# A hybrid decoder layer: the first tile of tokens gathers its own rows of U before it meets V densely

## The chip, the cores and the metric

The kernel runs on one NeuronCore of a Trainium2 chip. The metric is device microseconds from the first to the last instruction of one execution, as the median of timed runs. The engines are TensorE (PE in the profile, its weight loads PEld), VectorE (DVE), ScalarE (ACT), GpSimd (POOL) and SyncE (SP, which issues most DMAs).

## The reference, cut to what matters

The layer has two sub-layers over 512 tokens of width 1024. The first is token mixing by two groups of attention heads; the change doesn't touch it. The second is a retrieval over 128 x 128 = 16384 single-neuron experts:

```python
q = (hc @ w_q).reshape(-1, PEER_HEADS, PEER_KEY_DIM)     # 8 heads, 128 wide
s1 = einsum('chd,nd->chn', q[..., :half], k1)             # 128 keys on each side
s2 = einsum('chd,nd->chn', q[..., half:], k2)
v1, i1 = top_k(s1, 16); v2, i2 = top_k(s2, 16)
cand_s = v1[..., :, None] + v2[..., None, :]
best_s, best_pos = top_k(cand_s, 16)                      # 16 experts per head, 128 per token
expert = i1 * 128 + i2 at best_pos
g = softmax(best_s)
act = gelu(einsum('cd,chkd->chk', hc, u[expert]))         # rows of U
out = einsum('chk,chkd->cd', g * act, v[expert])          # rows of V
```

So each token uses 128 rows of U (16384 x 1024, f32) and the same 128 rows of V. The result, times a gate, is added to the residual and normalised.

## The kernel before, in words

The 512 tokens are four tiles of 128. Tiles 0, 1 and 2 are dense (`ND` = 3, `DT` = 384 tokens): for them every expert is computed and weighed by a gate matrix G that is zero where a token did not choose an expert. Tile 3 is sparse: for each of its 128 (head, choice) pairs an indirect DMA issued on GpSimd fetches one row of U per token, VectorE forms the dot product with the token's `h2n` row, and later a row of V is fetched and added into `acc0` on VectorE.

Every product in high precision is split into a high and a low float32r part (`hi` on ScalarE, `lo = raw - hi` on VectorE or GpSimd), and `mm3` (lines 147 to 150) issues three matmuls for each pair of operands.

The second sub-layer runs in this order:

1. Queries (`p_q`) of all tiles, and `route` (both sides' top 16 and the top 16 of their sums, on VectorE).
2. `choose` turns the lists into key numbers and gates (`sel3`). `spread` and `hot` (lines 781 to 816) build one-hot factors on VectorE, `gates` (line 820) multiplies them on TensorE into G and stores it to DRAM (`g_d`), 8 groups of 16 tokens for each of three dense tiles. Among these lie blocks of U: `u_block` (line 863) loads 128 experts' rows of U, splits them (`uhi`, `ulo`; `UPOOL` names the 14 blocks split on GpSimd), multiplies them with 384 tokens (24 matmuls of 128 x 384) and applies gelu. 56 blocks (`NAHEAD`) are done here; the first 16 (`NSPILL`) are written to DRAM, 40 stay in SBUF.
3. V, block by block (`v_load`, `v_mm`, lines 965 to 1004): 128 rows of V are split (`vhi`, `vlo`), the block's activations are weighed (`w = a * G`), split (`wh`, `wl`) and multiplied: 18 matmuls of 128 x 512 into six accumulators. From V block 16 on, one of the 72 remaining blocks of U goes with each block of V. The gathers of tile 3 are spread over the V blocks by the rates `RATE`: `due` counts up, and each whole number emits one gather with its VectorE operation.

The tile framework orders each engine's instructions once, when the program is built; `issue_after` keeps a gather's VectorE operation behind the last `wl`, and `high_priority` lets the load and the split of a block of U run ahead.

Of the kernel before, what the change touches and what calls it, by code (L numbers as in the profile page):

```python
# [9 lines left out]
F32 = mybir.dt.float32  # L10
# [47 lines left out]
UPOOL = tuple(range(0, 56, 4))  # L58
# [12 lines left out]
# columns of the small projection group  # L71
# [4 lines left out]
def hybrid_layer(ctx: ExitStack, tc, x, pos, wada, wada_n, cols, w_small, w_in_a, w_in_b, wuk, wuv,  # L76
# [19 lines left out]
    a_d = [dram.tile([P, DT], F32, name=f"a_d{b}") for b in range(NSPILL)]  # L96
# [70 lines left out]
    def row_out(s, pl, tag, bufs=1):  # L167
        """Section s of the modulation as one row in DRAM."""
# [22 lines left out]
    # ------------------------------------------------------------------ adaLN: mod = silu(c) @ w_ada + b_ada  # L191
# [17 lines left out]
    def mod_section(s, tiles, k0=0):  # L209
        """One section of the modulation; tiles holds [rows of w_ada's transpose, one column block each], loaded already or to load."""  # L210
# [10 lines left out]
    def mod_tiles(s, pl, tags, n, bufs=1):  # L221
        """The rows of a section, n blocks to a tile, with the tags in turn."""
# [7 lines left out]
    # the first two sections wait for their products where later tiles will lie; TensorE takes half of the first  # L230
# [12 lines left out]
    # x, normalised and transposed, before the modulation is known  # L243
# [44 lines left out]
    # ------------------------------------------------------------------ rotary tables  # L288
# [22 lines left out]
    def rope(v, nh, half, cs, sn, name):  # L311
        """v [P, NT, nh, >= 2*half], in place."""
# [12 lines left out]
    # ------------------------------------------------------------------ combined projection  # L325
# [69 lines left out]
    # queries, keys and values of group A; keys and values from the latent  # L395
# [26 lines left out]
    def forget():  # L422
        """Running sum of log sigmoid, as extra rows of keys and queries."""
# [30 lines left out]
    # queries, keys and values of group B  # L454
# [19 lines left out]
    # ------------------------------------------------------------------ attention  # L474
# [128 lines left out]
    # ------------------------------------------------------------------ group B, output projection, residual and PEER norm, tile by tile  # L603
# [19 lines left out]
    def peer_norm(j, x1):  # L623
        """h2 of tile j, transposed and split."""
# [19 lines left out]
    def h2_of(i, j):  # L644
        return h2l[0][:, i] if j == NT - 1 else h2[i][:, :, j * P:(j + 1) * P]
# [13 lines left out]
    for qt in range(NT):  # L659
# [4 lines left out]
        if qt == 1:  # L664
            h2 += [h2p.tile([P, KC, DT], F32R, tag=f"h2_{i}", name=f"h2_{i}") for i in range(2)]
# [8 lines left out]
    # ------------------------------------------------------------------ PEER: queries  # L674
    hp_ = opened(ctx, "hp")
    h2n = hp_.tile([P, D], F32, name="h2n")
    acc0 = hp_.tile([P, D], F32, name="acc0")
    g0 = hp_.tile([P, P], F32, name="g0")
    e0 = hp_.tile([P, P], U32, name="e0")
    w0 = hp_.tile([P, P], F32, name="w0")  # L680
    dot0 = hp_.tile([P, P], F32, name="dot0")
    if MB:
        row_out(5, hp_, "g4", 4)
    qT = [hp_.tile([P, PH, P], F32, tag="g4", name=f"qT{j}", bufs=4) for j in range(NT)]
    h2l.append(wo.tile([P, 2, KC, P], F32R, tag="mt", name="h2l", bufs=2))
    hf = peer_norm(NT - 1, x1s[NT - 1])
    for k4 in range(2):
        tp = one(f"tp_h2n{k4}")
        for k in range(4):
            nc.tensor.transpose(tp[:, k * P:(k + 1) * P], hf[:, k4 * 4 + k, :], ident)  # L690
        nc.scalar.activation(h2n[:, k4 * 512:(k4 + 1) * 512], tp, AF.Copy)
# [3 lines left out]
    # ------------------------------------------------------------------ PEER: product keys  # L695
# [6 lines left out]
    def route(n, j, idx, bval, bpos):  # L702
        """Product keys of heads 4n..4n+3 for the tokens of tile j."""
# [34 lines left out]
    def choose(j, idx, bval, bpos):  # L738
        """The two key numbers and the gate of each of the 128 (head, choice) pairs."""
# [41 lines left out]
    def spread(j, sel3):  # L781
        """One-hot factors: second key numbers as columns; first ones as 8 x 16, the gate in two parts on the 8."""
        i1 = rp.tile([P, 3, P], I32, tag="i1", name=f"i1_{j}")
        nc.vector.tensor_copy(i1[:, 0], sel3[:, 0])
# [5 lines left out]
        for i, src in enumerate((f1[:, 0], f1[:, 1], sel3[:, 1], sel3[:, 2])):  # L790
            nc.tensor.transpose(tp[:, i * P:(i + 1) * P], src, ident)
        tt = rp.tile([P, 5, P], F16, tag="tt", name=f"tt{j}")
        nc.scalar.activation(tt[:, 0:3], tp[:, 0:3 * P].rearrange("p (i t) -> p i t", t=P), AF.Copy)
        nc.scalar.activation(tt[:, 3], tp[:, 3 * P:4 * P], AF.Copy, scale=GSCALE)
        nc.vector.scalar_tensor_tensor(tt[:, 4], tp[:, 3 * P:4 * P], GSCALE, tt[:, 3], op0=ALU.mult, op1=ALU.subtract)
# [24 lines left out]
    def gates(j, tg, half, oh):  # L820
        """G[i2, i1, t] of these tokens; to DRAM 16 tokens at a time."""
# [3 lines left out]
        for t4 in range(2):  # L825
            o = one(f"p_g{j}_{tg}_{half}_{t4}", "pl")
            for t in range(4):
                q, e = divmod(t4 * 4 + t, 2)
                for i in (1, 0):
                    nc.tensor.matmul(o[:, t * P:(t + 1) * P], oh[2][:, q, :, e], oh[i][:, q, :, e],  # L830
                                     start=(t == 0 and i == 1), stop=i == 0, skip_group_check=True)
            ts_ = slice(half * 8 + t4 * 4, half * 8 + t4 * 4 + 4)
            nc.scalar.activation(st[:, :, ts_].rearrange("p i t -> p t i"), o.rearrange("p (t i) -> p t i", i=NK),  # L833
                                 AF.Copy, scale=1.0 / GSCALE)
# [5 lines left out]
    for n in range(2):  # L840
        his, los = wchunks(wo, [w_pq[n]], 512, f"pq{n}", 16, 2)
        for j in range(NT):
            o = one(f"p_q{n}_{j}", "pl")
            for k in range(KC):
                mm3(o, h2_of(0, j)[:, k], h2_of(1, j)[:, k], his[k], los[k], k == 0, k == KC - 1)
            qn = wo.tile([P, 512], F32, tag="x1", name=f"qn{n}_{j}", bufs=2)
            nc.scalar.activation(qn, o, AF.Copy)
            tp = one(f"tp_q{n}_{j}", "pj")
            for h in range(4):
                nc.tensor.transpose(tp[:, h * P:(h + 1) * P], qn[:, h * P:(h + 1) * P], ident)  # L850
# [268 lines left out]
```

## Time and profile before

| quantity | value |
|---|---|
| timed runs | 1632.31, 1643.91, 1644.44 us; median 1643.91 |
| span of the profiled execution | 1631.3 us (the profile gives no own time apart from the span; the lowest timed run is 1.0 us above it) |
| TensorE busy | 1549.9 us, 95% of the span |
| VectorE busy | 1273.8 us, 78% |
| ScalarE busy | 694.4 us, 43% |
| GpSimd busy | 538.3 us, 33% |
| moved by DMA | 383.39 MB, 235 GB/s over the span |
| mean granted TensorE clock | 0.967 of full speed |

Busy times of one engine can't be added to those of another, since the engines run side by side. Matmul records overlap each other, so the pace of TensorE is read from the distance between two starts, not from the length of a record; the same holds for VectorE, whose records overlap by some 0.08 us.

### The profile page before, as it was taken

To read this page: it belongs to the slowest core of one execution; us is meant where nothing else is said; L and a number is where in the kernel's file an instruction comes from. 1 tells how busy PE (TensorE), PEld (TensorE's weight loads), DVE (VectorE), ACT (ScalarE), POOL (GpSimd) and SP (SyncE) were. 2 spreads that over 40 slices of the span, in tenths; PEclk is the share of its full clock that TensorE was granted. 3 is DMA by queue.
4 is the path that set the end of the run, shared out by engine and by line. 5 is a ranking of instruction groups with operands and counts; after the bars stand their busy time and mean duration, and the time that the engine had idled before them with its cause. 6 is when DMAs were issued, how large, how long until landed. Compare 5 with 4: busy or idle time off the path is not lost.

```text
span 1631.3 us, 23016 instructions
## 1 busy us (share of the span) xinstructions
PE 1549.9 (95%) x8200; PEld 1348.3 (83%) x8202; DVE 1273.8 (78%) x2639; ACT 694.4 (43%) x1110; POOL 538.3 (33%) x406
## 2 busy tenths in 40 slices
PE   6889999998988998999999999999999999999997
PEld 5756777776788888888888999999999999988885
DVE  7898753655999999994468888878878888868886
ACT  4553434444334774865433333333333333333333
POOL 2344202213011202041005554555455445534420
PEclk7999898799999999999999999999999999999999
DMA  8643002413034655575889999989989899879974
GB/s 336 209 153 121 23 27 66 154 65 119 27 106 150 209 196 168 209 266 213 291 270 324 363 337 335 359 308 352 326 331 354 311 348 337 313 279 320 315 257 155
DMA packets 152899, 383.39 MB, mean 235 GB/s; under 512 B 11712, under 2 KB 66384, under 8 KB 149456
## 3 DMA queue, kind: packets, MB, share of 16 engines
q1 hardware_dynamic: 114912, 246.45, 44.3%
q0 software_dynamic: 36864, 134.23, 21.9%
q8 instruction: 64, 1.05, 0.3%
q10 hardware_dynamic: 1008, 1.24, 0.2%
q14 instruction: 51, 0.42, 0.1%
HBM read 349.36 MB, written 32.51 MB: 234 GB/s over the span
## 4 chain that ended last, share of the span: by engine, by line
PE 51%; DVE 3%; DMA 2%; issue 1%; ACT 1%; SPq 0%; POOL 0%; DVEq 0%; POOLq 0%; ACTq 0%
PE acc L1003 30%; PE p_u L150 7%; PE p_u L149 7%; PE p_u L148 7%; DMA ar<-a_d 1%; DVE gu L910 1%; DMA u<-in_ut_dram 1%; PE p_g L830 0%; DVE oh L814 0%; ACT st L833 0%; DMA v<-in_pv_dram 0%; DVE vlo L982 0%; DVE ulo L870 0%; DVE o L1024 0%; DVE x1b L1016 0%
## 5 line engine op out<-in xcount | busy, mean ns | idle before, releaser
L148 PE MATMUL p_u<-h,uhi 128*128 128x384 f32 x1024 | 349.1, 341 | 1.3 <-ACT a L876 1.3
L150 PE MATMUL p_u<-h,ulo 128*128 128x384 f32 x1024 | 348.6, 340 | 0.7 <-DVE ulo L870 0.6
L149 PE MATMUL p_u<-h,uhi 128*128 128x384 f32 x1024 | 348.1, 340 | 0.0
L902 POOL DMA_INDIRECT gu<-in_un_dram,e x128 | 192.0, 1500 | 297.3 <-DVE gu L910 203.5
L869 ACT ACTIVATE uhi<-u 128x1024 fp32r<-128x1024 f32 x128 | 135.8, 1061 | 292.3 <-PE p_u L149 247.6
L902 POOL DMA_INDIRECT gv<-in_pv_dram,e x128 | 191.7, 1498 | 205.2 <-DVE acc L921 155.2
L1003 PE MATMUL acc<-vhi,wh 128*128 128x512 f32 x768 | 237.3, 389 | 1.7 <-ACT wh L995 1.1
L1003 PE MATMUL acc<-vlo,wh 128*128 128x512 f32 x768 | 237.5, 389 | 0.8 <-DVE vlo L982 0.8
L1003 PE MATMUL acc<-vhi,wl 128*128 128x512 f32 x768 | 237.0, 389 | 0.0
L148 PEld LDWEIGHTS p_u<-h,uhi 128*128 128x128 f32 x1024 | 194.6, 190 | 4.7 <-ACT a L876 1.7
L149 PEld LDWEIGHTS p_u<-h,uhi 128*128 128x128 f32 x1024 | 195.0, 190 | 2.9
L150 PEld LDWEIGHTS p_u<-h,ulo 128*128 128x128 f32 x1024 | 194.7, 190 | 1.7 <-DVE ulo L870 1.0
L995 ACT ACTIVATE wh<-w 128x384 fp32r<-128x384 f32 x128 | 67.3, 526 | 299.9 <-issue 181.2
L996 DVE TENSOR_TENSOR wl<-w,wh 128x384 fp32r<-128x384 f32 x128 | 71.4, 558 | 136.7 <-ACT wh L995 136.6
L870 DVE TENSOR_TENSOR ulo<-u,uhi 128x1024 fp32r<-128x1024 f32 x114 | 139.0, 1219 | 48.9 <-ACT uhi L869 32.2
L1003 PEld LDWEIGHTS acc<-vlo,wh 128*128 128x128 f32 x768 | 144.0, 188 | 31.6 <-DVE vlo L982 1.7
L1003 PEld LDWEIGHTS acc<-vhi,wl 128*128 128x128 f32 x768 | 144.2, 188 | 29.9
L921 DVE SCALAR_TENSOR_TENSOR acc<-gv,w,acc 128x1024 f32<-128x1024 f32 x127 | 162.4, 1279 | 5.8 <-DMA gv<-in_pv_dram,e 5.5
L910 DVE SCALAR_TENSOR_TENSOR gu<-gu,h2n 128x1024 f32<-128x1024 f32 x128 | 158.6, 1255 | 9.7 <-DMA gu<-in_un_dram,e 9.7
L1003 PEld LDWEIGHTS acc<-vhi,wh 128*128 128x128 f32 x768 | 143.2, 188 | 26.7 <-ACT wh L995 1.4
L982 DVE TENSOR_TENSOR vlo<-v,vhi 128x1024 fp32r<-128x1024 f32 x128 | 156.1, 1220 | 5.0 <-ACT vhi L981 5.0
L981 ACT ACTIVATE vhi<-v 128x1024 fp32r<-128x1024 f32 x128 | 135.5, 1058 | 12.3 <-DMA v<-in_pv_dram 5.0
(356 smaller groups left out, 2396.3 us busy)
## 6 DMA issues: line engine op xcount, KB each, us to landing
u<-in_ut_dram SPq DMA_DIRECT2D x128, 512.0 KB, 5.3
v<-in_pv_dram SPq DMA_DIRECT2D x128, 512.0 KB, 5.9
g_d<-st SPq DMA_DIRECT2D x24, 1024.0 KB, 4.7
gt<-g_d SPq DMA_DIRECT2D x48, 512.0 KB, 8.8
wada<-in_wada_dram SPq DMA_DIRECT2D x12, 1024.0 KB, 4.9
raw_b<-in_w_in_b_dram SPq DMA_DIRECT2D x12, 512.0 KB, 3.6
x<-in_x_dram SPq DMA_DIRECT2D x8, 512.0 KB, 4.4
raw_o<-in_w_out_dram SPq DMA_DIRECT2D x8, 512.0 KB, 3.5
```

Of the source, the lines that this page charges most:

```text
L148: nc.tensor.matmul(o, ahi, bhi, start=start, stop=False, **kw)
L149: nc.tensor.matmul(o, ahi, blo, start=False, stop=False, **kw)
L150: nc.tensor.matmul(o, alo, bhi, start=False, stop=stop, **kw)
L869: nc.scalar.activation(hi, raw, AF.Copy)
L870: (nc.gpsimd if b in UPOOL else nc.vector).tensor_tensor(lo, raw, hi.bitcast(F32), op=ALU.subtract)
L902: nc.gpsimd.indirect_dma_start(out=t, out_offset=None, in_=src, in_offset=bass.IndirectOffsetOnAxis(ap=e0[:, s:s + 1], axis=0))
L910: nc.vector.scalar_tensor_tensor(t, t, 1.0, h2n, op0=ALU.mult, op1=ALU.mult, accum_out=dot0[:, s:s + 1])
L921: nc.vector.scalar_tensor_tensor(acc0, t, w0[:, s:s + 1], acc0, op0=ALU.mult, op1=ALU.add)
L981: nc.scalar.activation(hi, raw, AF.Copy)
L982: nc.vector.tensor_tensor(lo, raw, hi.bitcast(F32), op=ALU.subtract)
L996: last[0] = nc.vector.tensor_tensor(wl, w, wh.bitcast(F32), op=ALU.subtract).ins
L1003: nc.tensor.matmul(accs[2 * j + n], l[:, js], r[:, n * 512:(n + 1) * 512], start=b == 0 and i == 0, stop=b == NK - 1 and i == 2)
```

## The change

Tile 0 becomes half sparse. As soon as its experts are chosen, 128 indirect DMAs fetch its rows of U, VectorE forms the dots, and gelu and gate make `w0[0]`. Its matrix G then holds the finished weights, gate times activation, not the gates. So the dense products with U take tiles 1 and 2 alone (`UT` = 256 tokens), while V still meets tiles 0, 1 and 2. G of tile 0 is built last, from three bf16 parts in place of two f16 parts of the value. The queries are all computed before the blocks of U, tile 0 is routed first, and one more tile is routed among the blocks of U. 72 blocks of U are done ahead of V (`NSPILL` is 32). Half of the U splits (`UPOOL`, 64 of 128) and 30 of the V splits (`VPOOL`) go to GpSimd. In the V stage the weighing is done in place in the tile of G, and only for 256 tokens.

```diff
 ND = NT - 1
 DT = ND * P
+UT = DT - P
 NACT = 40
-NSPILL = 16
+NSPILL = 32
 NAHEAD = NACT + NSPILL
-WHEN = ((0, 2), (3, 5))
+WHEN = (1, 4)
-NGP = (0, 0, 0, 0, 1, 2, 3, 3)
+NGP = (1, 1, 2, 2, 2, 2, 2, 2)
-GPAT = (2, 2, 2, 2, 2, 2, 2, 2)
+GPAT = (3, 3, 3, 3, 3, 3, 3, 3)
+EARLY = (16, 6, 8)
-UPOOL = tuple(range(0, 56, 4))
+UPOOL = tuple(range(0, 128, 2))
+VPOOL = tuple(range(2, 120, 4))
...
+    query(0, 0)
+    route(0, 0, *lists[0])
+    query(1, 0)
+    route(1, 0, *lists[0])
+    query(0, 1)
+    query(1, 1)
+    sel3 = choose(0, *lists[0])
+    experts(0, sel3)
...
-        o = psum(f"p_u{b}")[:, :DT]
+        o = psum(f"p_u{b}")[:, :UT]
...
-        t = hp_.tile([P, D], F32, tag="g4", name=f"{name}{s}", bufs=4)
+        t = hp_.tile([P, D], F32, tag="g4", name=f"{name}{s}", bufs=6)
...
+    def dot(i, s, name):
+        t = gathered(un, i, s, name)
+        with tc.issue_after(last[0]) if last[0] is not None else nullcontext():
+            nc.vector.scalar_tensor_tensor(t, t, 1.0, h2n[i], op0=ALU.mult, op1=ALU.mult, accum_out=dot0[i][:, s:s + 1])
...
     u_ahead(U0[0])
+    dots(EARLY[0] // 2)
+    route(0, 1, *lists[1])
+    route(1, 1, *lists[1])
     u_ahead(U0[1])
+    dots(EARLY[0] // 2)
+    sel3 = choose(1, *lists[1])
...
+    for i, (j, coming) in enumerate(((1, 2), (2, 3), (0, None))):
+        if j == 0:
+            dots(TOPK)
+            weighed(0, slice(0, P))
+            tt = spread(0, sel0[:, 0], sel0[:, 1], w0[0])
+        else:
+            tt = spread(j, sel3[:, 0], sel3[:, 1], sel3[:, 2])
...
+                if tg == WHEN[0]:
+                    route(0, coming, *lists[coming])
+                    route(1, coming, *lists[coming])
...
+                dots(EARLY[1 + i])
             u_ahead(GPAT[tg])
...
-        nc.vector.tensor_tensor(lo, raw, hi.bitcast(F32), op=ALU.subtract)
-        w = vp.tile([P, DT], F32, tag="w", name=f"w{b}", bufs=2)
+        (nc.gpsimd if b in VPOOL else nc.vector).tensor_tensor(lo, raw, hi.bitcast(F32), op=ALU.subtract)
...
+        gw = gts[0][:, :, :, b % 8, :].rearrange("p j g t -> p (j g) t")
+        nc.vector.tensor_tensor(gw[:, P // 16:], a.rearrange("p (g t) -> p g t", t=16), gw[:, P // 16:], op=ALU.mult)
+        wh = vp.tile([P, DT], F32R, tag="wh", name=f"wh{b}", bufs=VB + 2)
...
```

## Rows read from the trace of the kernel before

**Rows 1.** Stretches; length; busy PE, PEld, DVE, ACT, POOL (count); clock, DMA share, GB/s.
```profile
410.00:720.00 310.00, 280.72 (x1860) 257.98 (x1859) 297.39 (x1155) 171.12 (x214) 49.29 (x38) 0.97 0.47 161
720.00:798.00 78.00, 72.29 (x516) 69.58 (x514) 38.58 (x50) 42.29 (x53) 12.71 (x6) 0.98 0.71 246
798.00:1457.00 659.00, 657.74 (x3294) 595.78 (x3295) 524.41 (x672) 235.85 (x323) 314.10 (x212) 1.00 0.92 329
1457.00:1592.00 135.00, 135.00 (x598) 111.81 (x597) 112.15 (x138) 50.06 (x68) 51.14 (x31) 1.00 0.83 285
1592.00:1631.00 39.00, 28.97 (x125) 22.90 (x123) 26.99 (x46) 13.62 (x27) 2.22 (x4) 0.94 0.48 159
```
**Rows 2.** The chain that ended last: start, length, what; two rounds in the V stage.
```profile
961.04 4.08 PE acc L1003 x18
969.30 4.08 PE acc L1003 x18
```
**Rows 3.** Timeline of TensorE in a block of U: start, length, line, operation.
```profile
702.23 0.33 PE L150 MATMUL p_u<-h,ulo 128*128 128x384 f32 x1
...
702.75 0.33 PE L150 MATMUL p_u<-h,ulo 128*128 128x384 f32 x1
```
**Rows 4.** Timeline of TensorE where two matmuls of 256 columns follow each other.
```profile
284.35 0.27 PE L524 MATMUL pl<-kbt,qt 64*128 64x256 f32 x1
284.46 0.27 PE L525 MATMUL pl<-kbt,qt 64*128 64x256 f32 x1
```
**Rows 5.** Timeline of VectorE in the V stage with a block of U.
```profile
1001.13 1.22 DVE L910 SCALAR_TENSOR_TENSOR gu<-gu,h2n 128x1024 f32<-128x1024 f32 x1
...
1002.28 1.22 DVE L910 SCALAR_TENSOR_TENSOR gu<-gu,h2n 128x1024 f32<-128x1024 f32 x1
...
1003.42 1.22 DVE L870 TENSOR_TENSOR ulo<-u,uhi 128x1024 fp32r<-128x1024 f32 x1
```
**Rows 6.** Groups of VectorE by line and form: count, busy us, mean ns, idle before.
```profile
L921 DVE SCALAR_TENSOR_TENSOR acc<-gv,w,acc 128x1024 f32<-128x1024 f32 x127 | 162.4, 1279 | 5.8 <-DMA gv<-in_pv_dram,e 5.5
L814 DVE TENSOR_TENSOR oh<-o,o 128x1024 f16<-128x1024 f16 x96 | 62.8, 681 | 0.0
L282 DVE TENSOR_TENSOR hm<-xT,hm 128x256 fp32r<-128x256 f32 x16 | 6.3, 416 | 0.1
```
**Rows 7.** Groups of GpSimd by line, from 410 to 798 us, columns as in rows 6.
```profile
L870 POOL TENSOR_TENSOR ulo<-u,uhi 128x1024 fp32r<-128x1024 f32 x14 | 35.5, 2535 | 158.7 <-ACT uhi L869 158.6
L902 POOL DMA_INDIRECT gu<-in_un_dram,e x13 | 18.5, 1424 | 69.5 <-DVE i L786 27.5 <-PE p_u L148 22.4 <-DVE wk L717 16.4
```
**Rows 8.** Timeline: splits on GpSimd and what VectorE did meanwhile.
```profile
476.19 2.39 POOL L870 TENSOR_TENSOR ulo<-u,uhi 128x1024 fp32r<-128x1024 f32 x1 [9.33 <-ACT uhi L869]
...
477.51 0.27 DVE L718 MAX8 v<-wk 128x8 f32<-128x128 f32 x1
...
545.48 2.57 POOL L870 TENSOR_TENSOR ulo<-u,uhi 128x1024 fp32r<-128x1024 f32 x1 [17.24 <-ACT uhi L869]
...
545.71 2.49 DVE L770 TENSOR_TENSOR eq<-eq 128x256 f16<-128x256 f16 x1
...
696.69 2.75 POOL L870 TENSOR_TENSOR ulo<-u,uhi 128x1024 fp32r<-128x1024 f32 x1
...
697.11 3.42 DVE L910 SCALAR_TENSOR_TENSOR gu<-gu,h2n 128x1024 f32<-128x1024 f32 x1
```
**Rows 9.** Timeline of VectorE late in the V stage, no U block.
```profile
1500.83 0.55 DVE L988 TENSOR_TENSOR w<-a,gt 128x384 f32<-128x384 f32 x1
...
1502.11 0.56 DVE L996 TENSOR_TENSOR wl<-w,wh 128x384 fp32r<-128x384 f32 x1 [0.72 <-ACT wh L995]
1502.58 1.28 DVE L921 SCALAR_TENSOR_TENSOR acc<-gv,w,acc 128x1024 f32<-128x1024 f32 x1
```
**Rows 10.** DMA from 798 to 1631 us: rate in 40 slices; one kind of issue.
```profile
GB/s 296 307 236 304 333 350 398 321 360 346 305 346 361 300 345 359 288 325 377 343 282 387 323 301 384 320 292 362 354 305 323 238 290 341 333 296 343 189 147 156
...
v<-in_pv_dram SPq DMA_DIRECT2D x125, 512.0 KB, 5.8
```

More of the change, by code (lines that the diff above doesn't have):

```diff
@@ L95, in hybrid_layer @@
     x1_d = [dram.tile([P, D], F32, name=f"x1_d{j}") for j in range(NT)]
-    a_d = [dram.tile([P, DT], F32, name=f"a_d{b}") for b in range(NSPILL)]
+    a_d = [dram.tile([P, UT], F32, name=f"a_d{b}") for b in range(NSPILL)]
     g_d = [dram.tile([P, P // 16, NK, 16], F32, name=f"g_d{j}") for j in range(ND)]
@@ L664, in hybrid_layer @@
         if qt == 1:
-            h2 += [h2p.tile([P, KC, DT], F32R, tag=f"h2_{i}", name=f"h2_{i}") for i in range(2)]
+            h2 += [h2p.tile([P, KC, UT], F32R, tag=f"h2_{i}", name=f"h2_{i}") for i in range(2)]
+            h2e = h2p.tile([P, 2, KC, P], F32R, name="h2e")
         if qt > 0:
@@ L675, in hybrid_layer, with natural @@
     hp_ = opened(ctx, "hp")
-    h2n = hp_.tile([P, D], F32, name="h2n")
+    h2n = [hp_.tile([P, D], F32, name=f"h2n{i}") for i in range(2)]
     acc0 = hp_.tile([P, D], F32, name="acc0")
[L678 to L681, printed above, removed]
+    g0, w0, dot0 = ([hp_.tile([P, P], F32, name=f"{n_}{i}") for i in range(2)] for n_ in ("g", "w", "dot"))
+    e0 = [hp_.tile([P, P], U32, name=f"e{i}") for i in range(2)]
+    sel0 = hp_.tile([P, 2, P], F32, name="sel0")
     if MB:
-        row_out(5, hp_, "g4", 4)
-    qT = [hp_.tile([P, PH, P], F32, tag="g4", name=f"qT{j}", bufs=4) for j in range(NT)]
-    h2l.append(wo.tile([P, 2, KC, P], F32R, tag="mt", name="h2l", bufs=2))
[L686 to L691, printed above, removed]
+        row_out(5, hp_, "g4", 6)
+    qT = [hp_.tile([P, PH, P], F32, tag="g4", name=f"qT{j}", bufs=6) for j in range(NT)]
+    def natural(i, hf):
+        for k4 in range(2):
+            tp = one(f"tp_h2n{i}_{k4}")
+            for k in range(4):
+                nc.tensor.transpose(tp[:, k * P:(k + 1) * P], hf[:, k4 * 4 + k, :], ident)
+            nc.scalar.activation(h2n[i][:, k4 * 512:(k4 + 1) * 512], tp, AF.Copy)
+    hf0 = hp_.tile([P, KC, P], F32, tag="g4", name="hf0", bufs=6)
+    nc.vector.tensor_tensor(hf0, h2e[:, 0].bitcast(F32), h2e[:, 1].bitcast(F32), op=ALU.add)
+    natural(0, hf0)
+    h2l.append(wo.tile([P, 2, KC, P], F32R, tag="mt", name="h2l", bufs=2))
+    natural(1, peer_norm(NT - 1, x1s[NT - 1]))
     rt = ExitStack()
@@ L789, in spread @@
         tp = one(f"tp_s{j}")
-        for i, src in enumerate((f1[:, 0], f1[:, 1], sel3[:, 1], sel3[:, 2])):
+        for i, src in enumerate((f1[:, 0], f1[:, 1], n2, val_)):
             nc.tensor.transpose(tp[:, i * P:(i + 1) * P], src, ident)
[L792 to L795, printed above, removed]
@@ L803, in spread @@
+        for i in range(n):
+            nc.vector.tensor_tensor(o8[i], o8[n - 1], pairs(tv[:, i], 8), op=ALU.mult)
         return tt, o16, o8
@@ L828, in gates @@
                 q, e = divmod(t4 * 4 + t, 2)
-                for i in (1, 0):
-                    nc.tensor.matmul(o[:, t * P:(t + 1) * P], oh[2][:, q, :, e], oh[i][:, q, :, e],
-                                     start=(t == 0 and i == 1), stop=i == 0, skip_group_check=True)
+                for i in reversed(range(len(oh))):
+                    nc.tensor.matmul(o[:, t * P:(t + 1) * P], oh2[:, q, :, e], oh[i][:, q, :, e],
+                                     start=(t == 0 and i == len(oh) - 1), stop=i == 0, skip_group_check=True)
             ts_ = slice(half * 8 + t4 * 4, half * 8 + t4 * 4 + 4)
             nc.scalar.activation(st[:, :, ts_].rearrange("p i t -> p t i"), o.rearrange("p (t i) -> p t i", i=NK),
-                                 AF.Copy, scale=1.0 / GSCALE)
+                                 AF.Copy, scale=1.0 / GSCALE if j else 1.0)
         if half == 1:
@@ L839, in hybrid_layer, with query, experts @@
               rp.tile([P, PH, PK], U32, name=f"bpos{j}")) for j in range(NT)]
[L840 to L850, printed above, removed]
-            nc.scalar.activation(qT[j][:, 4 * n:4 * n + 4, :], tp.rearrange("p (h t) -> p h t", t=P), AF.Copy)
-            if n == 0 and j >= RLAG:
-                route(n, j - RLAG, *lists[j - RLAG])
-        for j in range(NT - RLAG if n == 0 else NT, NT):
-            route(n, j, *lists[j])
+    wpq = [wchunks(wo, [w_pq[n]], 512, f"pq{n}", 16, 2) for n in range(2)]
+    def query(n, j):
+        his, los = wpq[n]
+        o = one(f"p_q{n}_{j}", "pl")
+        for k in range(KC):
+            mm3(o, h2_of(0, j)[:, k], h2_of(1, j)[:, k], his[k], los[k], k == 0, k == KC - 1)
+        qn = wo.tile([P, 512], F32, tag="x1", name=f"qn{n}_{j}", bufs=2)
+        nc.scalar.activation(qn, o, AF.Copy)
+        tp = one(f"tp_q{n}_{j}", "pj")
+        for h in range(4):
+            nc.tensor.transpose(tp[:, h * P:(h + 1) * P], qn[:, h * P:(h + 1) * P], ident)
+        nc.scalar.activation(qT[j][:, 4 * n:4 * n + 4, :], tp.rearrange("p (h t) -> p h t", t=P), AF.Copy)
+    def experts(i, sel3):
+        nc.vector.scalar_tensor_tensor(e0[i], sel3[:, 0], float(NK), sel3[:, 1], op0=ALU.mult, op1=ALU.add)
+        nc.vector.tensor_copy(g0[i], sel3[:, 2])
+    query(0, 0)
[6 more added lines that the diff above has]
+    experts(0, sel3)
+    nc.scalar.activation(sel0, sel3[:, 0:2], AF.Copy)
+    for j in (2, 3):
+        for n in range(2):
+            query(n, j)
     wst.close()
@@ L874, in u_block @@
         spilt = b < NSPILL
[L875 removed]
+        a = up.tile([P, UT], F32, tag="as" if spilt else "a", name=f"a{b}", bufs=2 if spilt else NACT)
         nc.scalar.activation(a, o, AF.Gelu)
```

115 lines of the change are left out of this document (58 added, 57 removed).

## Prediction

> **What bounds the kernel now.** I read the busy times by stretch first, then the chain that ended last, then the timeline of VectorE and GpSimd inside each stage. The stretches [rows 1] show three regimes. From 410 to 720 us (queries, routing, one-hot factors) VectorE is busy 297 of 310 us, so it sets the pace, though TensorE is well filled too. From 720 to 798 VectorE is half idle and TensorE finishes its blocks of U. From 798 to 1592 TensorE is never idle at a granted clock of 1.00, and the chain is matmuls alone: a round of one V block and one U block takes 969.30 - 961.04 = 8.26 us [rows 2], of which V's 18 matmuls are 4.13. But VectorE is close behind: 524 of 659 us, and the DMA engines are 0.92 busy. So removing TensorE work pays only in the V stage, and only as far as VectorE, GpSimd and DMA allow.
>
> **The change, part by part.**
>
> *U's products.* Matmuls of 384 columns start (702.75 - 702.23)/3 = 0.173 us apart [rows 3]; two of 256 columns start 0.11 apart [rows 4], and by columns it would be 0.115, which I take. A block of U costs TensorE 24 x 0.115 = 2.76 us in place of 4.13, so 128 blocks give back 175 us of TensorE. G of tile 0 with three factors adds 128 small matmuls, under 10 us. This is the whole gain, and it counts only where TensorE stays the bound.
>
> *Before V (410 to 798 now).* VectorE's busy time there is 297 + 39 = 336 us [rows 1]. Added on the same engine: 128 dots. Their records last 1.22 us but start 1.15 apart [rows 5], so 147 us. None of this can be moved behind the start of V, for G of tile 0 needs all 128 dots and is built last in this stage. 16 more one-hot products at 0.6 to 0.68 [rows 6] are 10 us, the split parts and the sum for `h2n` 2, five more of tile 3's gathers (14 instead of 9) 6. Removed: of 72 blocks of U 36 are split on VectorE, of 56 it was 42, so six splits at 1.14 [rows 5], 7 us.
>
> *Splits on GpSimd.* The timeline shows what such a split does to VectorE [rows 8]. While GpSimd's split runs from 696.69 to 699.44, a dot that starts at 697.11 takes 3.42 us in place of 1.22; while one runs from 545.48 to 548.05, a small f16 sum takes 2.49. Both end only after the split has ended, which is a stall of about 2.2 us. A MAX8 at 477.51 inside another split takes its ordinary 0.27. So an operation of VectorE with two tensor inputs in SBUF stands still for the rest of the split; a search over a single one doesn't. A split costs VectorE 1.14 us if it does it itself and up to 2.2 if GpSimd does it (2.5 us there [rows 7]). Of the 14 such splits now, 8 (two stand in rows 8) met such an operation and cost VectorE 18 us together. With 36 splits, and dots and one-hots as the main work, I charge 56 us in all, 38 more (bounds: 15 more, if they fall among the routing as half do now; 61 more, if every one costs 2.2).
>
> The Trainium skill has a rule on this (GPSIMD Engine Reference, section Specifications): GpSimd shares its SBUF interfaces with VectorE and contends with VectorE instructions that have two SBUF inputs or run in a two-port mode. It speaks against this change, and the trace agrees with the 3.42 us above.
>
> The sum for VectorE before V is 336 + 147 + 10 + 2 + 6 - 7 + 38 = 532 us, and at its present 96% of the time 554 us. TensorE is busy 281 + 72 = 353 us there now [rows 1], 56 x 4.13 = 231 of it for U; with 72 x 2.76 = 199 in their place it needs some 320 of the 554, so it waits. GpSimd has 36 x 2.5 + 142 gathers x 1.42 = 292 us [rows 7] and is covered, though a gather waiting for a free buffer holds up the splits and index casts behind it. V then starts at 410 + 554 = 964 in place of 798: 166 us lost before the first block of V.
>
> *The V stage.* 56 blocks of U are left (72 before), and 242 gathers (256 less 14). The rates sum to 32 x 0.2 + 56 x 2.75 + 36 x 1.1 = 200, and 242 x 1.02 / 200 = 1.23, so three phases have 0.25, 3.39 and 1.36 gathers a round.
>
> Phase one, 32 blocks of V alone: TensorE's 4.13 us bound it, 132 us. VectorE needs about 3.2.
>
> Phase two, 56 rounds with U: TensorE needs 4.13 + 2.76 = 6.89. VectorE needs 0.75 V splits and 0.5 U splits at 1.14 (1.42 us), the weighing of 256 columns at 0.35 (0.416 less the overlap [rows 6]), `wl` 0.47 and the wait for `wh` ahead of it 0.72 [rows 9], and 3.39 gathers at 1.15 to 1.20 [rows 5, 9], 3.97 us: 6.93 together. To this come 0.75 splits on GpSimd at 2.2, another 1.65, less what falls into the wait for `wh`. This is 8.2 to 8.6 us, and I take 8.5. That price lies between nothing (no split on GpSimd in this stage is in the trace) and 1.65. DMA gives a second floor: a round moves V, U (each 512 KB), G (192 KB) and 3.39 rows of 512 KB, 3.02 MB. At the 357 GB/s that the present stage gives when its engines are fully busy (329 at 0.92 [rows 1]) that is 8.4 us; at the best slice, 398 GB/s [rows 10], 7.6. GpSimd itself needs 0.75 x 2.5 + 3.39 x 1.42 = 6.7. So 56 x 8.5 = 476 us.
>
> Phase three, 33 rounds up to the tail: VectorE 0.78 x 1.14 + 0.35 + 0.72 + 0.47 + 1.36 x 1.2 = 4.06 us and 0.22 x 2.2 = 0.5 of stall, 4.5 against TensorE's 4.13: 149 us. The tail stays at 39 us [rows 1].
>
> V stage: 132 + 476 + 149 + 39 = 796 us, against 833 now. Of the 175 us given back by TensorE, 37 reach the end.
>
> *Parts with one answer.* The spill of 32 blocks (128 KB each) in place of 16 (192 KB) adds 1 MB each way, 3 us of DMA beside 4.13 us rounds that aren't DMA-bound. The weighing in place and the larger buffers remove no wait on the chain. Routing tile 0 first moves VectorE work, it adds none. SP's loads of U come earlier in phase one and have room. Up to 410 us nothing changes.
>
> **Sum.** 410 + 554 + 796 = 1760 us of span, against the profiled span of 1631. The timed runs lie 1 to 13 us above that span, so I predict **1765 us**, 7% above the median of 1643.9.
>
> **The rivals.**
>
> *The stall doesn't count in the V stage* (and little before it): GpSimd's splits fall into VectorE's waits. For it: VectorE waits 0.72 us in each round anyway; against: a split lasts 2.5. Then before V takes 494/0.96 = 515 us, phase two is bound by DMA at 8.4 (471), phase three by TensorE (136), and the sum is 410 + 515 + 132 + 471 + 136 + 39 = 1703; with 398 GB/s it is 1658. Chance 0.18.
>
> *Faster than before:* phase two runs at TensorE's 6.9 us. It needs the splits and the two-input operations of VectorE to run side by side at full rate and DMA to give 3.02 MB / 6.9 us = 438 GB/s. Then 410 + 515 + 132 + 386 + 136 + 39 = 1618. The turning point is 7.1 us a round, where the sum is the span of now. For it, the slices above 380 GB/s; against it, no slice reaches 400 [rows 10] and the stalls are in the trace. Chance 0.10, with some overlap between engines that I count too low.
>
> The Trainium skill's DMA: Bandwidth & Descriptors (section Where 436 GB/s comes from) gives about 358 GB/s as one core's share of HBM and 435 as the fabric's limit. Slices at 398 pass the first, and the second would allow 6.9 us a round.
>
> *Worse:* VectorE's fixed order waits for gathers that are stuck on GpSimd behind a split that waits for ScalarE, since both queues are in order; and TensorE, half idle before V, falls to its lower clock (it was granted 0.97 there with few gaps [rows 1]). With 0.88 of the time used before V (605 us) and 9.3 us a round (521), the sum is 410 + 605 + 132 + 521 + 155 + 39 = 1862. Chance 0.10.
>
> *The change does only part of what it says:* tile 0's dots could be spread into VectorE's idle 39 us after 720. They fill it in my sum already, so this gives no other time.
>
> **How the numbers follow.** My forecast has 0.62, the rivals 0.18, 0.10 and 0.10. The range leaves out the faster and the worse one: from 1650 (the first rival with the best DMA rate) to 1830 (all of the stalls charged, 554 grown to 580 and 9 us a round). The timed runs of the kernel before differ by 0.7%, so 1% is about what can be told from no change. Slower by over 1% has 0.83, within 1% 0.07 (the low end of the first rival), faster 0.10.
>
> **What would show it.** The first matmul of V starts near 960 us; VectorE is over 93% busy from 430 us to there, TensorE some 60%. U's matmuls start 0.115 us apart where they run freely. In rounds with U the period is 8 to 9 us and TensorE shows gaps, with waits on `vlo`, `ulo` and `wl`. Two-input operations of VectorE last above 3 us beside splits on GpSimd. I am wrong if V starts before 900 us, if rounds with U take under 7.5 us, or if the two-input operations keep their 1.22 us beside GpSimd's splits.

## The result, and the profile after

The changed kernel takes 1869.39 us (median of four, 1866.44 to 1874.93) against 1638.11 for the kernel before on the same chip: a ratio of 1.143, 95% interval 1.139 to 1.147. I had predicted 1765 with a range up to 1830. The side was right; the time is 104 us above the forecast and 39 above the top of the range.

The span is 1867.2 us, 235.9 more than before. The first V matmul starts at 1023.7 us (799.0 before, 964 predicted), so 224.7 us of the loss lie ahead of V and only 11.2 in the V stage. These stretches of the changed kernel answer [rows 1], with the same columns:

```profile
410.00:720.00 310.00, 229.41 (x1527) 206.60 (x1525) 274.38 (x919) 121.88 (x170) 148.37 (x97) 0.87 0.64 213
720.00:1023.00 303.00, 176.66 (x1436) 165.83 (x1436) 259.74 (x568) 117.07 (x142) 163.50 (x108) 0.76 0.79 282
1023.00:1180.00 157.00, 148.72 (x626) 119.98 (x627) 98.68 (x144) 55.91 (x77) 50.87 (x28) 0.97 0.80 257
1180.00:1677.00 497.00, 400.20 (x2258) 343.99 (x2258) 410.41 (x459) 149.88 (x216) 368.93 (x224) 0.93 0.92 329
1677.00:1830.00 153.00, 143.59 (x608) 116.95 (x607) 110.91 (x131) 50.77 (x67) 76.56 (x42) 0.97 0.79 262
1830.00:1867.00 37.00, 26.12 (x112) 20.40 (x110) 22.64 (x38) 11.97 (x24) 2.21 (x4) 0.91 0.48 157
```

Read the third number group (VectorE) against the length. Ahead of V it is busy 274 + 260 = 534 us. That is the 532 of my sum, but they take 613 us, 87% of the time, not the 96% that I used. From 1180 to 1677, where blocks of U go along with V, no engine is full: TensorE 400 of 497, VectorE 410, DMA 0.92. Something stands between them, and the waits of VectorE in the V stage name it (total, times, longest):

```profile
DVE gt L1041 <- DMA gt<-g_d: 74.8, 11, 13.3
DVE wl L1045 <- ACT wh L1044: 66.3, 44, 4.2
DVE gu L938 <- DMA gu<-in_un_dram,e: 18.6, 15, 3.2
```

The first is new; the kernel before has no wait for `g_d` at all. Its two longest in the V stage are these (the wait for `wh` is even longer there, but TensorE was full and lost nothing by it):

```profile
DVE wl L996 <- ACT wh L995: 136.6, 107, 5.0
DVE gu L910 <- DMA gu<-in_un_dram,e: 9.7, 13, 1.3
```

TensorE now waits in turn for the low parts of V that VectorE makes; in the kernel before, this wait is 0.8 us:

```profile
PE acc L1053 <- DVE vlo L1035: 78.9, 23, 10.2
```

The chain that ended last (start, length, what) shows what it does to the rounds, which in [rows 2] were matmuls alone:

```profile
1419.48 17.69 DMA gt<-g_d
...
1482.86 4.14 PE acc L1053 x18
...
1495.23 17.86 DMA gt<-g_d
...
1698.43 9.56 DMA gt<-g_d
...
1735.29 11.22 DMA gt<-g_d
...
1774.77 10.49 DMA gt<-g_d
```

And the timeline of VectorE shows why it waits, beside a stretch that runs freely (compare [rows 5]):

```profile
1424.70 1.21 DVE L938 SCALAR_TENSOR_TENSOR gu<-gu,h2n 128x1024 f32<-128x1024 f32 x1
1425.85 0.08 DVE L938 DVE_READ_ACCUMULATOR gu<-gu,h2n 128x1 f32 x1
1437.30 2.77 DVE L1041 TENSOR_TENSOR gt<-a,gt 128x256 f32<-128x256 f32 x8 [11.38 <-DMA gt<-g_d]
1439.99 0.56 DVE L1045 TENSOR_TENSOR wl<-gt,wh 128x384 fp32r<-128x384 f32 x1
```

VectorE stands 11.38 us, then weighs eight blocks in a row, a whole group of G (other groups come in runs of two to eight). Only the first of the eight is needed soon. The engine takes its instructions in the written order, so `vlo`, `ulo` and the gathers' sums wait behind them.

Ahead of V, the waits of VectorE from 460 us on are for rows of U that tile 0 gathers and for `uhi`:

```profile
DVE gd L938 <- DMA gd<-in_un_dram,e: 36.1, 19, 5.2
DVE ulo L907 <- ACT uhi L906: 22.8, 13, 8.8
```

The stall beside GpSimd's splits is there as in [rows 8]; the two timelines side by side, GpSimd first:

```profile
653.31 2.35 POOL L907 TENSOR_TENSOR ulo<-u,uhi 128x1024 fp32r<-128x1024 f32 x1
```
```profile
653.55 3.21 DVE L938 SCALAR_TENSOR_TENSOR gd<-gd,h2n 128x1024 f32<-128x1024 f32 x1 [1.06 <-DMA gd<-in_un_dram,e]
```

In the groups over the whole span, `acc` has gone from 1279 ns [rows 6] to 1532 and a GpSimd split from 2535 [rows 7] to 2624:

```profile
L907 POOL TENSOR_TENSOR ulo<-u,uhi 128x1024 fp32r<-128x1024 f32 x64 | 167.9, 2624 | 67.6 <-ACT uhi L906 66.5
L956 DVE SCALAR_TENSOR_TENSOR acc<-gv,w,acc 128x1024 f32<-128x1024 f32 x127 | 194.6, 1532 | 8.0 <-DMA gv<-in_pv_dram,e 7.3
```

TensorE's side came as worked out. U's matmuls of 256 columns in the V stage start 0.11 to 0.12 us apart ([rows 3]: 0.173 with 384):

```profile
1246.55 0.28 PE L150 MATMUL p_u<-h,uhi 128*128 128x256 f32 x1
1246.66 0.28 PE L151 MATMUL p_u<-h,uhi 128*128 128x256 f32 x1
1246.78 0.28 PE L152 MATMUL p_u<-h,ulo 128*128 128x256 f32 x1
```

### The profile page after: what moved, and what is told of

Same layout as the page of the kernel before. It is cut to its first block, busy times and chain, and to the rows that moved or that the text cites. A ratio compares the mean times of both kernels' runs of the same rounds, so it can differ in the third digit from the quotient of the medians.

```text
span 1867.2 us, 23863 instructions
## 1 busy us (share of the span) xinstructions
PE 1497.0 (80%) x8336; PEld 1260.3 (67%) x8338; DVE 1448.6 (78%) x2837; ACT 685.0 (37%) x1113; POOL 918.6 (49%) x614
## 4 chain that ended last, share of the span: by engine, by line
PE 30%; DVE 22%; issue 17%; DMA 16%; POOL 11%; ACT 3%; SPq 1%; POOLq 0%; DVEq 0%; ACTq 0%
PE acc L1053 11%; DMA gt<-g_d 4%; DMA gd<-in_un_dram,e 3%; POOL gu L932 3%; DMA u<-in_ut_dram 3%; POOL ulo L907 3%; PE po L551 2%; POOL gv L932 2%; DMA gv<-in_pv_dram,e 2%; DVE oh L836 2%; DVE acc L956 2%; DVE gd L938 2%; DVE ulo L907 1%; DMA v<-in_pv_dram 1%; POOL gd L932 1%
## 5 line engine op out<-in xcount | busy, mean ns | idle before, releaser
L152 PE MATMUL p_u<-h,ulo 128*128 128x256 f32 x1024 | 313.3, 307 | 115.7 <-DVE ulo L907 63.9
L150 PE MATMUL p_u<-h,uhi 128*128 128x256 f32 x1024 | 308.2, 301 | 27.6 <-ACT uhi L906 26.4
L151 PE MATMUL p_u<-h,uhi 128*128 128x256 f32 x1024 | 306.0, 299 | 0.0
L150 PEld LDWEIGHTS p_u<-h,uhi 128*128 128x128 f32 x1024 | 212.1, 207 | 34.3 <-ACT uhi L906 30.5
L932 POOL DMA_INDIRECT gd<-in_un_dram,e x128 | 172.2, 1345 | 127.9 <-DVE gd L938 50.9
L151 PEld LDWEIGHTS p_u<-h,uhi 128*128 128x128 f32 x1024 | 211.7, 207 | 2.5
L907 POOL TENSOR_TENSOR ulo<-u,uhi 128x1024 fp32r<-128x1024 f32 x64 | 167.9, 2624 | 67.6 <-ACT uhi L906 66.5
L956 DVE SCALAR_TENSOR_TENSOR acc<-gv,w,acc 128x1024 f32<-128x1024 f32 x127 | 194.6, 1532 | 8.0 <-DMA gv<-in_pv_dram,e 7.3
L938 DVE SCALAR_TENSOR_TENSOR gu<-gu,h2n 128x1024 f32<-128x1024 f32 x128 | 183.2, 1449 | 19.0 <-DMA gu<-in_un_dram,e 19.0
L938 DVE SCALAR_TENSOR_TENSOR gd<-gd,h2n 128x1024 f32<-128x1024 f32 x128 | 168.8, 1346 | 36.2 <-DMA gd<-in_un_dram,e 36.1
L1044 ACT ACTIVATE wh<-gt 128x384 fp32r<-128x384 f32 x128 | 66.9, 524 | 288.1 <-PE acc L1053 276.2
L855 ACT ACTIVATE st<-p_g 128x512 f32<-128x512 f32 x96 | 95.1, 1091 | 137.5 <-PE p_g L852 117.7
```

The costliest lines, as they stand in the source:

```text
L150: nc.tensor.matmul(o, ahi, bhi, start=start, stop=False, **kw)
L151: nc.tensor.matmul(o, ahi, blo, start=False, stop=False, **kw)
L152: nc.tensor.matmul(o, alo, bhi, start=False, stop=stop, **kw)
L907: (nc.gpsimd if b in UPOOL else nc.vector).tensor_tensor(lo, raw, hi.bitcast(F32), op=ALU.subtract)
L932: nc.gpsimd.indirect_dma_start(out=t, out_offset=None, in_=src, in_offset=bass.IndirectOffsetOnAxis(ap=e0[i][:, s:s + 1], axis=0))
L938: nc.vector.scalar_tensor_tensor(t, t, 1.0, h2n[i], op0=ALU.mult, op1=ALU.mult, accum_out=dot0[i][:, s:s + 1])
```

## The experiments

My theory after the result had three parts: the dots and their gathers ahead of V cost more than VectorE's busy time; GpSimd's splits stall VectorE; and the weighing in place lets VectorE run into G that has not been loaded. The rivals were that gathers are held up behind splits in GpSimd's queue, that TensorE's lower clock holds the stretch ahead of V, and that the transfers bound the V stage anyway. The table gives the first V matmul, the V stage (span less that start) and the median with its ratio to the kernel before on the same chip, whose median there was 1630.0 to 1639.0 us. The first two columns are read from one profiled execution of each run, so differences of a few us between them count for little: e2, which changes next to nothing ahead of V, starts V 5.2 us earlier. e3, e4, e9 and e11 leave work out and do not compute the layer; they price a part and are no kernels to use.

| run | first V matmul | V stage | time | ratio (95%) |
|---|---|---|---|---|
| before | 799.0 | 832.3 | 1638.11 | |
| changed | 1023.7 | 843.5 | 1869.39 | 1.143 (1.139 to 1.147) |
| e1_splits_back | 1032.2 | 779.3 | 1811.54 | 1.105 (1.101 to 1.109) |
| e2_gt_early | 1018.5 | 845.0 | 1864.80 | 1.138 (1.134 to 1.141) |
| e3_no_dots | 842.6 | 851.2 | 1697.95 | 1.036 (1.031 to 1.040) |
| e4_dots_resident | 973.4 | 838.3 | 1814.64 | 1.107 (1.103 to 1.111) |
| e5_weigh_in_turn | 1023.4 | 784.2 | 1808.56 | 1.109 (1.103 to 1.114) |
| e6_turn_splits_back | 1029.2 | 768.1 | 1793.84 | 1.100 (1.090 to 1.109) |
| e7_before_gpsimd | 817.5 | 838.5 | 1657.13 | 1.016 (1.011 to 1.021) |
| e8_before_in_place | 802.1 | 857.4 | 1659.08 | 1.017 (1.011 to 1.023) |
| e9_no_dots_best_v | 825.3 | 763.2 | 1590.89 | 0.974 (0.967 to 0.981) |
| e10_fine_dots | 1009.9 | 845.8 | 1857.18 | 1.137 (1.129 to 1.145) |
| e11_half_gathers | 992.2 | 848.6 | 1838.42 | 1.126 (1.116 to 1.136) |
| e12_all_repairs | 1015.6 | 767.1 | 1788.55 | 1.093 (1.087 to 1.099) |

**e1_splits_back.**

```diff
-UPOOL = tuple(range(0, 128, 2))
-VPOOL = tuple(range(2, 120, 4))
+UPOOL = tuple(range(0, 56, 4))
+VPOOL = ()
```

> GpSimd splits as few as before the change: every 4th U block up to 56 on GpSimd, no V block; all the rest of the change stays. If the splits' cost is the stall of VectorE, then acc (1532 ns), gu (1477 ns) and wl (642 ns) go back to about 1280, 1220 and 560 ns, but VectorE gets back some 56 splits of 1.22 us in the V stage, 68 us for about 60 us of stalls: rounds of phase two stay between 8.5 and 9.0 us, the first V matmul comes at 1000 to 1015 (18 more splits are 22 us, less 38 us of stalls), and the time is 1845 to 1875. If the greater cost is that gathers stand in GpSimd's queue behind the splits, the rounds fall below 8.3 and the time below 1820. If the splits on GpSimd help after all, the time is over 1890.

The durations went back as expected (`acc` 1282 ns, `gu` 1222, `wl` 556), but the first V matmul came 17 us after the expected range, and the V stage fell by 64 us, which looks like the rival. It isn't clean evidence, though: with other splits the written order is another one. In the rounds with U no more than five weighings stand in a row, where there were up to eight, and the waits for G fell from 74.8 to 24.1 us. VectorE's longest waits in this run:

```profile
DVE ulo L907 <- ACT uhi L906: 84.0, 32, 10.9
DVE wl L1045 <- ACT wh L1044: 45.6, 37, 1.9
DVE gd L938 <- DMA gd<-in_un_dram,e: 34.9, 22, 4.5
DVE gt L1041 <- DMA gt<-g_d: 24.1, 6, 9.4
```

Ahead of V nothing was gained (1032.2 against 1023.7), and the wait for gathered rows is the same 35 us with 14 splits on GpSimd as with half of all blocks. So the added splits on GpSimd don't hold the gathers up there. e5 and e6 separate the rest.

**e2_gt_early.**

```diff
-        if b % 8 == 0:
-            gt = vp.tile(... name=f"gt{b}", bufs=2)
+        if b == 0 or b % 8 == 4 and b + 8 < NK + 4:
+            bg = 0 if b == 0 else b + 4
+            gt = vp.tile(... name=f"gt{bg}", bufs=2)
...
-            gts[0] = gt
+            gts[bg // 8] = gt
...
```

> The loads of G for the next 8 blocks are issued 4 blocks earlier in SP's queue; nothing else is changed. If the 75 us that VectorE stands for G are a loss of their own, the wait of the weighing for g_d is nearly gone, a round of phase two falls from 8.87 to about 7.9 us, phase three by 8 us, and the time is 1795 to 1815. If another limit (VectorE's own work, or the transfers at 329 GB/s) stands right behind, the same time comes back as waits for vlo, ulo or u, and the kernel ends above 1850.

Neither. The wait for G stayed:

```profile
DVE gt L1042 <- DMA gt<-g_d: 74.7, 11, 11.2
DVE wl L1046 <- ACT wh L1045: 67.0, 42, 4.2
```

The load of G still starts when the buffer of the group before last comes free: the last `wl` of group 7 ends at 1404.7 us, and the load of group 9 is issued at 1404.8. The weighings are written close behind that point. Moving the load in the program moves neither. What is left to change is the place of the weighings.

**e3_no_dots and e4_dots_resident.** The first leaves out the dots and their gathers, the second the gathers alone.

```diff
+    nc.vector.memset(dot0[0], 0.0)      # e3
     def dots(n):
-        for _ in range(min(n, TOPK - nd[0])):
+        for _ in range(0):
...
     def dot(i, s, name):                # e4
-        t = gathered(un, i, s, name)
+        t = gathered(un, i, s, name) if i else hp_.tile([P, D], F32, tag="g4", name=f"{name}{s}", bufs=6)
+        if i == 0:
+            nc.vector.scalar_tensor_tensor(t, h2n[0], 1.0, h2n[0], op0=ALU.mult, op1=ALU.mult, accum_out=dot0[i][:, s:s + 1])
+            return
```

> Leaves out the first tile's 128 gathers and dot products (its dots are zero); its G and all the rest are built. If VectorE's work before V sets that stretch, its 169 us of dots and 36 us of waits for them go and the first V matmul comes at 820 to 860 in place of 1023.7; the stage of V is as long as now (835 to 850) and the time is 1660 to 1700. If the low clock of TensorE or the U loads set the stretch, the first V matmul comes after 900 and the time is above 1740.

> The first tile's 128 dot products stay on VectorE, but each multiplies a row block that already lies in SBUF: the 128 gathers (67 MB of transfers and 172 us of GpSimd's issuing) are left out. If VectorE's work alone sets the stretch before V, only the 36 us of waits for gathered rows go, and part of the waits that GpSimd's late splits cause: first V matmul at 970 to 1000, time 1810 to 1845. If the gathers' transfers and their place in GpSimd's queue set it, the first V matmul comes before 940 and the time is below 1790.

Both came out inside the first theory's numbers, but for e3's V stage, which is 1.2 us over. The stretch from 410 us to the first V matmul, columns as above; first the changed kernel:

```profile
410.00:1023.70 613.70, 406.09 (x2964) 372.46 (x2962) 534.57 (x1487) 239.58 (x313) 311.87 (x204) 0.82 0.71 247
```

e3:

```profile
410.00:842.60 432.60, 351.38 (x2955) 326.03 (x2954) 379.98 (x1229) 234.56 (x311) 144.82 (x75) 0.95 0.56 194
```

and e4:

```profile
410.00:973.40 563.40, 391.61 (x2962) 360.22 (x2962) 526.92 (x1486) 239.33 (x310) 141.74 (x75) 0.85 0.45 150
```

The dots alone make the stretch 973.4 - 842.6 = 130.8 us longer, the gathers another 1023.7 - 973.4 = 50.3 (none predicted). In VectorE's busy time the dots are 526.92 - 379.98 = 146.9 us, the 147 of the prediction; 16 of them fill time in which VectorE was idle in e3. Of the 50.3 us of the gathers, 36.1 are the waits for rows above and 534.57 - 526.92 = 7.7 longer busy time. In e4 VectorE is busy 527 of 563 us, 94%, and the stretch is 50 us shorter at a granted clock of 0.85, little above the 0.82 of the changed kernel; without the dots (e3) the clock is 0.95. So the low clock goes along with TensorE's waits for VectorE, and isn't what sets the stretch.

**e5_weigh_in_turn and e6_turn_splits_back.**

```diff
+        with tc.issue_after(last[0]) if last[0] is not None else nullcontext():
-        nc.vector.tensor_tensor(gw[:, P // 16:], a..., gw[:, P // 16:], op=ALU.mult)
+            nc.vector.tensor_tensor(gw[:, P // 16:], a..., gw[:, P // 16:], op=ALU.mult)
```

e6 has the two lines of e1 as well.

> Each weighing in place is put behind the wl of the block before in VectorE's order, so that VectorE can no longer run through a whole group of 8 weighings ahead; the splits stay as changed. Loading G earlier in the program had moved nothing, since the order written down put those 8 weighings at the moment when the buffer comes free. If VectorE stands for G only because the weighings run ahead, the 75 us of waits for g_d fall under 10 us, the V stage goes from 843 to 775 to 800 us and the time to 1800 to 1825. If something else ends as late (splits, transfers), the V stage stays above 830 and the time above 1850.

> Weighings in turn, and the splits on GpSimd as few as before the change. Against the run with the splits alone put back (1811.5 us, where 24 us of waits for G were left), the waits for G should go: 1785 to 1800. The distance to the run with the weighings in turn and the splits on GpSimd is then the price of the stalls by themselves: about 0 to 30 us if a GpSimd split costs VectorE as much as doing it itself does, over 45 us if GpSimd's queue, with the gathers behind the splits, is the greater loss.

In e5 no wait for `g_d` is left on VectorE in the V stage, and the stage falls by 59.3 us, the time by 60.8 (1869.39 to 1808.56). This one edit puts each weighing back in its turn. The longest waits of the V stage are now:

```profile
DVE wl L1046 <- ACT wh L1045: 79.8, 80, 2.6
DVE gt L1042 <- DMA ar<-a_d: 6.8, 2, 5.0
```

With the weighings in turn, putting the splits back is worth 784.2 - 768.1 = 16.1 us in the V stage, not 64. That is inside the 0 to 30 us expected if GpSimd's queue is not the greater loss, and a rough price: the two runs of e6 lie 10.5 us apart. What the stage comes up against is seen in the stretch from U's first to its last matmul behind the start of V. The DMA engines are 0.99 busy in it, with the splits on GpSimd (e5, first) as without (e6), and in e1 too, at 373 GB/s:

```profile
1176.70:1623.80 447.10, 394.82 (x2252) 338.31 (x2251) 422.49 (x450) 145.47 (x216) 353.79 (x223) 0.98 0.99 364
1174.40:1603.00 428.60, 392.51 (x2233) 342.78 (x2231) 367.95 (x463) 146.70 (x211) 238.38 (x176) 0.95 0.99 365
```

**e7_before_gpsimd and e8_before_in_place.** One part of the change at a time, put into the kernel before.

```diff
-UPOOL = tuple(range(0, 56, 4))          # e7
+UPOOL = tuple(range(0, 128, 2))
+VPOOL = tuple(range(2, 120, 4))
-        nc.vector.tensor_tensor(lo, raw, hi.bitcast(F32), op=ALU.subtract)
+        (nc.gpsimd if b in VPOOL else nc.vector).tensor_tensor(lo, raw, hi.bitcast(F32), op=ALU.subtract)
...
-        w = vp.tile([P, DT], F32, tag="w", name=f"w{b}", bufs=2)     # e8
+        w = gts[0][:, :, :, b % 8, :].rearrange("p j g t -> p (j g) t")
...
```

> The kernel before with the changed kernel's lists of splits on GpSimd (64 blocks of U, 30 of V) and nothing else. Here TensorE is the bound in the V stage, with VectorE at 0.80. If a split on GpSimd stops VectorE's two-input operations, acc goes from 1279 to about 1500 ns, TensorE waits for vlo and ulo, and the time is 1655 to 1700. If the splits only take load off VectorE, acc stays at 1279 ns and the time is 1625 to 1642.

> The kernel before with the weighing done in place in the tile of G (no tile w, all 384 columns as before) and nothing else. If weighing in place alone makes the order run ahead, weighings of up to 8 blocks stand side by side on VectorE, waits for g_d of 30 to 75 us appear where there were none, and the time is 1650 to 1700. If the waits come only with the other parts of the change (more transfers, a later G), the time stays within 10 us of 1638.

e7 takes 1.6% longer (interval 1.1 to 2.1), and its `acc` is stalled as in the changed kernel:

```profile
L922 DVE SCALAR_TENSOR_TENSOR acc<-gv,w,acc 128x1024 f32<-128x1024 f32 x127 | 194.2, 1529 | 25.3 <-DMA gv<-in_pv_dram,e 24.5
```

But the place was not the one expected: 18.5 us are lost ahead of V and 6.2 in the V stage, and these behind the rounds with U, which take 8.23 us as against 8.22 before. That fits stalls that fall into VectorE's idle time there, which no run shows directly. e8 (1.7% longer, interval 1.1 to 2.3) shows the other effect by itself. The kernel before had no wait for `g_d`; now there is one, and the V stage is 25.1 us longer:

```profile
DVE wl L995 <- ACT wh L994: 60.0, 46, 2.7
DVE gt L988 <- DMA gt<-g_d: 58.8, 11, 8.2
```

**e9_no_dots_best_v.** The edits of e3 and e6 together: what is left of the change is, in the main, U's products for 256 tokens, with the first tile's dots left out.

> Leaves out the first tile's 128 gathers and dots (its dots are zero), with the weighings in turn and the splits put back on VectorE: what is left of the change is U's products for 256 tokens. The stretch before V should end at 835 to 850 as without the dots (842.6), the V stage take 768 us as with the other two repairs (1797.3 less 1029.2), together 1605 to 1620, under the 1638 of the kernel before. If the products' smaller width were itself a loss (TensorE at a lower clock, weight loads that no longer hide), the time is above 1640.

It is faster than the kernel before, by 44 us (1.9 to 3.3%), and 14 us better than the expected range. The gain on TensorE is real, and with the V stage repaired the whole of the loss hangs on the dots and their gathers: e12 less e9 is 198 us, 190 of them ahead of V.

**e10_fine_dots and e11_half_gathers.** What the 50 us of the gathers are.

```diff
                 waiting.append((j, tg, half, *hot(j, tg, half, *tt)))    # e10
+                if coming is not None and half == 0:
+                    dots(EARLY[1 + i] // 2)
...
-                dots(EARLY[1 + i])
+                dots(EARLY[1 + i] - EARLY[1 + i] // 2)
```

e11 takes e4's edit for odd `s` alone.

> The dots of the first tile are emitted in halves, 3 or 4 after each half of the one-hot factors, in place of 6 or 8 after both; nothing else is changed. If VectorE waits for gathered rows (36 us before V) because 6 or 8 dots in a row outrun six buffers, these waits fall below 15 us and the first V matmul comes at 995 to 1010. If the rows come late because of the transfers (gathers and U blocks together at 250 to 286 GB/s) or of GpSimd's queue, it stays at 1015 to 1030 and the time within 1 per cent of 1868.

> Every second dot of the first tile works on a row block that already lies in SBUF, so 64 of its 128 gathers are left out and the 128 dots on VectorE stay. With all gathers the first V matmul came at 1023.7, with none at 973.4. If the 50 us are a cost of each gather, it comes at 995 to 1002. If they arise only where the supply is outrun, half the gathers already bring nearly all of it: 973 to 985.

e10 comes out at the edge of its first case: the wait for gathered rows falls from 36.1 to 17.1 us and the first V matmul comes 13.8 us earlier, so runs of 6 or 8 dots do outrun the six buffers:

```profile
DVE gd L938 <- DMA gd<-in_un_dram,e: 17.1, 14, 2.8
```

e12 against e6, with the same edit, gives 13.6 us. In e11, with half of the gathers, it comes 31.5 us earlier, between the two expectations and nearer to a cost of each gather. So about 14 of the 50 us are runs, and some 36 are not split any further.

**e12_all_repairs.** The edits of e6 and e10 together, with four timed runs (1777.33 to 1793.55 us).

> The three repairs together on the changed kernel: weighings in turn, the splits put back on VectorE, the first tile's dots in halves. If they add up, the first V matmul comes at about 1015 (1029 with the splits back, less 14 for the finer dots), the V stage takes 765 to 770 us and the time is 1775 to 1788, still 8 to 9 per cent above the kernel before: the 128 dots on VectorE ahead of V cost more than all of the rest. If the losses hide one another, the time stays near 1794.

They add up in the trace (1015.6 and 767.1); the median is 0.6 us above the expected range. The best form of this change that I found is 9% slower than the kernel before, so none beats both.

## Why the prediction was right and wrong

- **U's products: right.** Starts 0.115 us apart were predicted, 0.11 to 0.12 are in the rows. e9 shows that part of the gain reaches the end where nothing else eats it: 44 of the 175 us that TensorE gives back.
- **VectorE's busy time ahead of V: right, 532 us against 534.** Its parts hold too: the dots are 146.9 us (147 predicted), all else that the change adds 379.98 - 336.38 = 43.6 (49 predicted).
- **"At its present 96% of the time 554 us": the step that failed first, 60 us.** The 0.96 is that of 410 to 720 us in [rows 1], for work with hardly a gather in it; over the whole stretch up to V the kernel before had 336 of 389, 0.86. My sum let the dots fill that idle time, and they nearly do when their rows are resident: 94%, 9 us behind the forecast (e4). But the dots bring their own supply, 128 transfers of 512 KB, and I gave it no price beside GpSimd's busy time. With the gathers the share is 87%. So the sum needed a term of some 50 us for them. The rival "worse" had 605 us for this stretch and 9.3 us a round, near the 614 and 9.2 measured. Part of that is luck: VectorE does wait for gathers, but e1 shows that fewer splits on GpSimd don't shorten that wait, and it had no place for the weighing.
- **"The weighing in place and the larger buffers remove no wait on the chain": the step that failed second, 59 us.** True as it stands, and the wrong question: the edit adds a wait. The tile `w` with its two buffers was what kept a weighing near its block. Without it the written order puts up to a whole group's weighings at the point where G could be there, and VectorE stands until it is (e5, e8).
- **The stall beside GpSimd: mechanism right, its price in the V stage not measured by itself.** Two-input operations do stand for the rest of a split (3.21 us above). The Trainium skill (SBUF — State Buffer, section SBUF: two separate sides) calls it an exclusive lock, held for the whole instruction; the rows agree, and it is stronger than the contention that I had cited. I took 8.5 us a round, 1.57 of them for the stall. Once the wait for G is gone, a round of phase two takes 8.24 us with the splits on GpSimd (e5) and 7.99 without (e6), both inside the 7.6 to 8.4 that I gave as the floor by DMA, and the DMA engines are 0.99 busy in both. So little is to be gained by taking the splits away; ahead of V it is 17 us without the dots (e3 against e9) and none with them (e1).
- **Phase two at 8.5 us a round.** By the starts of V's blocks, the changed kernel took 139.8 us for phase one, 512.8 for phase two, 9.16 a round, and 190.9 for the rest, against 132, 476 and 188 predicted. (U's matmuls span 494.8 us there for 54 blocks; two of the 56 had run ahead of V.) The two mistakes partly offset each other: the weighing adds 59.3 us, and without it the V stage takes 784.2 (e5), 11.8 less than my 796, which leaves the 47.5 that I was short. The Trainium skill (DMA: Bandwidth & Descriptors, section Where 436 GB/s comes from) has about 358 GB/s, half of a stack's bandwidth, as what binds a core's transfers from HBM. The 365 over 428.6 us in e6 is slightly above it, and the measurement decides.
- **The faster rival** needed 6.9 us a round; no run has come under 7.8.
- **TensorE's clock** did fall ahead of V (0.82 over the stretch, 0.97 before). e3 and e4 speak for a consequence.

The books for the span: 130.8 for the dots, 50.3 for their gathers and 43.6 for the rest ahead of V (e3 less before), together 224.7. Of the 43.6, 17.3 go with GpSimd's splits (e3 less e9), and the other 26.3 stand beside 373 us of VectorE in e9 against 336. In the V stage a gain of 64.2 (e6 less before) is given back by 59.3 for the order of the weighings and 16.1 for the splits, which leaves 11.2. The last two shares depend on which is undone first: with the splits first, which changes the order too, they are 64.2 (e1) and 11.2 (e6 less e1), for either repair alone brings the rounds with U to the point where DMA is full.

Open: which share of the 36 us that remain with each gather belongs to the transfers, to GpSimd's issuing, or to U's loads beside them. That DMA bounds the repaired rounds is read from its busy share of 0.99; no run takes transfers out of the V stage to test it.

## What to carry to other kernels

When work moves to an engine that is already the bound of a stage, add up its busy time, and then give the supply of that work its own price: here the dots made the stretch 131 us longer and their rows another 50. When a buffer is dropped because its data can live in another one, ask which order the buffer enforced; on an engine that takes instructions in a fixed order, work allowed to run ahead is work that can stand in front of everything else. And a change of splits that shifts the written order also moves other waits, so undo one thing with the order held before reading a price from it.

## What was not expected of the hardware

The DMA engines kept 0.99 busy at 365 GB/s over 428.6 us of V and U blocks with gathers among them, where [rows 10] show single slices between 236 and 398 up to the last block of U. And with the DMA engines that full, 56 splits (26 of U, 30 of V) moved from GpSimd to VectorE change the V stage by only 16 us, though each can hold up a two-input operation for some 2 us.
